# A decoder trunk with forgetting attention: norms of four token tiles at once, operand preparation in another place, masks first in their banks

## The chip, the cores and the metric

The kernel runs on one core of one Trainium2 chip. The metric is the device time of one execution in microseconds (us); smaller is better. All inputs are fp32, and the arithmetic keeps close to fp32: a dense product is emulated by three matmuls in a faster float form.

## The reference

```python
for l in range(DEPTH):                      # 2 layers, x is 512 tokens x 1024
    x = x + 0.5 * swiglu(rms_norm(x, ffn1_norm[l]), ffn1_w_in[l], ffn1_w_out[l])
    h = rms_norm(x, mix_norm[l]) @ w_mix_in[l]
    (c_x, c_b, c_c, h_q, h_f, h_i, h_g, f_q, f_k, f_v, f_f) = jnp.split(h, split_at, axis=-1)
    y = jnp.concatenate([
        short_conv_mixer(c_x, c_b, c_c, conv_w[l]),
        hgrn2_mixer(h_q, h_f, h_i, h_g, lower_bounds[l], hgrn_out_gain[l]),
        fox_mixer(f_q, f_k, f_v, f_f, fox_f_bias[l], fox_q_gain[l], fox_k_gain[l]),
    ], axis=-1)
    x = x + y @ w_mix_out[l]
    x = x + 0.5 * swiglu(rms_norm(x, ffn2_norm[l]), ffn2_w_in[l], ffn2_w_out[l])
...
# fox_mixer: 8 heads of 64, blocks of 128 queries
qh = rms_norm(heads(q), q_gain) * (HEAD_DIM ** -0.5)
kh = rms_norm(heads(k), k_gain)
cum = jnp.cumsum(jax.nn.log_sigmoid(f_logit + f_bias), axis=1)
s = einsum('bhqd,bhkd->bhqk', qb, kh) + (cb[..., :, None] - cum[..., None, :])
s = jnp.where(qpos[:, None] >= kpos[None, :], s, MASK_VALUE)
o = einsum('bhqk,bhkd->bhqd', jax.nn.softmax(s, axis=-1), vh)
```

The change touches `fox_mixer` alone: the norms of its queries and keys, the making of a head's operands, and the place of the causal mask within the scores.

## The kernel before

Each layer runs `ffn`, `mix`, `ffn`. A dense product splits both sides into a high and a low part (on the weights' side ACT casts the high part at L435, DVE takes the remainder at L438; buffers `st` for the weights as they come, two of them, and `hl` for the parts, three), and `mm3` issues three matmuls: high by high (L451), high by low (L457), low by high (L458). ACT is ScalarE, DVE VectorE, PE TensorE, POOL GpSimd, SP the engine whose queue issues most transfers.

`mix` has two stages that matter here.

In the first one two generators of `hgrn` (one for each pair of heads) run in turn with dense steps of `fox_qkv`; the table `HGRN_BESIDE` says how many dense steps stand between two steps of `hgrn`. `hgrn` computes its scores in three groups of levels: 64 small matmuls in `score` (L1494) write two banks tagged `sc`, DVE's `place` copies them under a mask into the matrix `A` (L1514), and before these copies it makes the operands of the next group (L1463, L1464, L1471). `fox_qkv` projects the queries and keys of four heads for one half `hf` of the heads, then of the other half, each into four banks (one for each tile of 128 tokens), copies a bank to `qk` (L1661) and queues one call of `norm(qk, i)` for each token tile in `later`. `beside` pops one such call after each dense step. `norm` takes the sum of squares of 8 vectors of 64 in each token row (Square on ACT at L1644, reduction on DVE at L1645), the inverse root by Ln and Exp on ACT and a correcting step (`rsqrt`, L597, L600, L601; with two scalings, L1646 and L1652), all on 128x8 elements, and scales the tile (L1655).

In the second stage `fox_attend` walks through 16 steps (h, p): head h, first (p = 0) or second (p = 1) half of the query blocks. A step does, before the change, in this order:

- `turn(h, p)`: transposes the weights of the step (3 blocks for p = 0, 7 for p = 1; L1772) into `pt` banks; ACT casts them to PH (L1777), DVE takes the remainder PL (L1778);
- `scores` of the step two ahead: for each query block a matmul of QA with KA and one of QB with KB into a bank `sc` (in these two matmuls lie the parts of the split and the two rows for the decay), and the causal mask, a bf16 matmul of an identity with `maskb`, added to the same bank (all L1735); then the maximum (L1749), Exp (L341), reciprocal (L1751) and the scaling of the weights (on ACT L1755 for p = 1, on DVE L1757 for p = 0);
- `values` of the step before: PH and PL against V into the one bank `po` (L1790); for p = 1 also the sum into `fo` (L1803, L1804), and for an odd head the parts `fyh` on ACT (L1807) and `fyl` on DVE (L1808), operands of the output projection;
- for p = 0, `prep` of head h + 2 (`fox_prep`): a two-row transfer (L1693), a POOL memset (L1694), four transposes of `qk` into a `pt` bank (L1697), the high part `hi` on ACT (L1700), the low part `lo` on DVE (L1701), and six transfers on SP that put their 64-row halves together to QA, KA, QB, KB (L1708).

Heads alternate between two sets of these operands: `S`, `q` for odd ones, `A`, `kb` for even ones. Between the steps run dense ones (the V and conv projections and most of the output projection), as many as the table `BESIDE` says. There are two banks `pt`, two `sc`, one `po`.

On PE `self.follow("p")` fixes the order of the matmuls of these steps as the program writes them. On the other engines the instructions stand in the order that a scheduler gives them, with what the program writes first ahead where both can go. Each engine then works its queue off in order.

## Time and profile before

| | |
|---|---|
| three runs | 1764.95, 1764.04, 1764.25 us; median 1764.25 |
| the profiled execution's own time | 1765.45 us |
| its span in the profile | 1763.3 us |
| granted TensorE clock | 1.00 of full speed |
| first stage of `mix`, layer 0 / layer 1 | about 384 to 446 / 1250 to 1318 us |
| second stage (`fox_attend`) | about 446 to 558 / 1318 to 1430 us |
| PE busy in these four stretches | 61.77 of 62, 110.86 of 112, 67.77 of 68, 111.55 of 112 us |

In the rows below a line such as L1735 is a line of the kernel before; buffer numbers are left out of names. "sc<-q,q" means that the instruction reads two buffers q and writes the bank sc. "PEld" is PE's loading of weights, which overlaps the matmuls. PE's matmuls are pipelined: a row's duration is longer than the distance to the next start, and that distance is what the matmul costs. A bracket behind a row is the idle time ahead of it and what ended it.

### The profile page before, as it was taken

The numbers are of one execution on the slowest core, as the hardware profiler recorded it, in microseconds if no ns is written. First come the engines' busy times: TensorE is split into PE (matmuls) and PEld (weight loads), VectorE is DVE, ScalarE is ACT, GpSimd is POOL, SyncE is SP. The second block draws the span as 40 slices with busy tenths as digits, with TensorE's granted clock in tenths as the row PEclk, the third lists the DMA queues.
The fourth block names the chain that finished last, engine by engine and source line by source line (L and its number), as shares of the span: only waits on it lengthen the run. The fifth ranks groups of instructions, "written<-read, shape, count | busy, mean of one in ns | idle before, by whom it ended". The sixth has DMA issues, their size and how long they took to land.

```text
span 1763.3 us, 33430 instructions
## 1 busy us (share of the span) xinstructions
PE 1753.8 (99%) x13613; PEld 1643.2 (93%) x13613; DVE 1416.0 (80%) x1956; ACT 1015.8 (58%) x1433; POOL 177.0 (10%) x174
## 2 busy tenths in 40 slices
PE   9999999999999999999999999999999999999999
PEld 7999999888888899999989999998888889999998
DVE  7988788679777898888679787876888779888783
ACT  5465555466666565555446656555657655655652
POOL 0011120100000111112001111201000001120200
PEclk9999999999999999999999999999999999999999
DMA  7768784243543776869267787923435438687762
GB/s 202 188 140 199 180 177 111 73 124 82 132 118 99 216 163 161 202 169 178 81 183 170 178 182 176 192 79 79 120 93 134 123 103 220 156 176 195 162 138 96
DMA packets 257465, 262.34 MB, mean 149 GB/s; under 512 B 25832, under 2 KB 236528, under 8 KB 257312
## 3 DMA queue, kind: packets, MB, share of 16 engines
q1 hardware_dynamic: 201456, 192.02, 36.4%
q0 software_dynamic: 55840, 68.19, 24.0%
q8 instruction: 107, 1.75, 0.4%
q14 instruction: 46, 0.38, 0.1%
q10 hardware_dynamic: 16, 0.00, 0.0%
HBM read 226.15 MB, written 2.17 MB: 129 GB/s over the span
## 4 chain that ended last, share of the span: by engine, by line
PE 90%; DVE 6%; ACT 2%; issue 1%; DMA 1%; SPq 0%; ACTq 0%; DVEq 0%
PE mm L451 12%; PE mm L458 12%; PE mm L457 12%; PE sc L458 6%; PE sc L451 6%; PE sc L457 6%; PE pt L457 6%; PE pt L451 6%; PE pt L458 6%; PE po L451 3%; PE po L458 3%; PE po L457 3%; DVE hl L438 1%; PE sc L1735 1%; PE po L1790 1%; PE pt L1772 1%
## 5 line engine op out<-in xcount | busy, mean ns | idle before, releaser
L916 DVE TENSOR_TENSOR hl<-w,hl 128x1024 fp32r<-128x1024 f32 x279 | 341.0, 1223 | 91.0 <-ACT hl L914 89.5
L914 ACT CAST hl<-w 128x1024 fp32r<-128x1024 f32 x279 | 292.6, 1049 | 198.3 <-PE mm L458 56.0
L438 DVE TENSOR_TENSOR hl<-st,hl 128x1024 fp32r<-128x1024 f32 (+3 forms) x152 | 160.4, 1056 | 103.0 <-ACT hl L435 101.4
L435 ACT CAST hl<-st 128x1024 fp32r<-128x1024 f32 (+3 forms) x151 | 137.4, 910 | 160.9 <-PE po L458 61.7
L451 PE MATMUL mm<-xc,hl 128*128 128x256 f32 x698 | 191.6, 275 | 0.6 <-ACT u L1034 0.6
L458 PE MATMUL mm<-xc,hl 128*128 128x256 f32 x696 | 191.6, 275 | 0.0
L457 PE MATMUL mm<-xc,hl 128*128 128x256 f32 x696 | 191.5, 275 | 0.0
L451 PE MATMUL pt<-xc,hl 128*128 128x256 f32 x546 | 149.7, 275 | 0.0
L457 PE MATMUL pt<-xc,hl 128*128 128x256 f32 x544 | 149.7, 275 | 0.0
L458 PE MATMUL pt<-xc,hl 128*128 128x256 f32 x544 | 149.6, 275 | 0.0
L451 PEld LDWEIGHTS mm<-xc,hl 128*128 128x128 f32 x698 | 133.9, 192 | 0.9 <-ACT u L1034 0.8
L458 PEld LDWEIGHTS mm<-xc,hl 128*128 128x128 f32 x696 | 133.6, 192 | 0.4 <-DVE hl L916 0.4
L457 PEld LDWEIGHTS mm<-xc,hl 128*128 128x128 f32 x696 | 133.6, 192 | 0.0
L458 PE MATMUL sc<-xc,hl 128*128 128x256 f32 x464 | 127.8, 275 | 0.1
L451 PE MATMUL sc<-xc,hl 128*128 128x256 f32 (+1 forms) x466 | 127.8, 275 | 0.0
L457 PE MATMUL sc<-xc,hl 128*128 128x256 f32 x464 | 127.7, 275 | 0.0
L451 PE MATMUL mm<-x,hl 128*128 128x512 f32 x272 | 105.9, 390 | 0.0
L451 PEld LDWEIGHTS pt<-xc,hl 128*128 128x128 f32 x546 | 104.7, 192 | 0.0
L457 PEld LDWEIGHTS pt<-xc,hl 128*128 128x128 f32 x544 | 104.4, 192 | 0.0
L458 PEld LDWEIGHTS pt<-xc,hl 128*128 128x128 f32 x544 | 104.4, 192 | 0.0
L457 PE MATMUL mm<-x,hl 128*128 128x512 f32 x272 | 103.1, 379 | 0.0
L458 PE MATMUL mm<-x,hl 128*128 128x512 f32 x272 | 103.1, 379 | 0.0
(520 smaller groups left out, 5595.9 us busy)
## 6 DMA issues: line engine op xcount, KB each, us to landing
w<-in_ffn_w_in_dram SPq DMA_DIRECT2D x124, 512.0 KB, 6.0
w<-in_ffn_w_out_dram POOLq DMA_DIRECT2D x50, 512.0 KB, 9.6
w<-in_ffn_w_out_dram SPq DMA_DIRECT2D x49, 512.0 KB, 4.5
st<-in_ffn_w_out_dram SPq DMA_DIRECT2D x39, 512.0 KB, 3.8
st<-in_w_mix_in_dram SPq DMA_DIRECT2D x72, 256.0 KB, 3.0
st<-in_ffn_w_in_dram SPq DMA_DIRECT2D x70, 256.0 KB, 3.5
w<-in_ffn_w_in_dram POOLq DMA_DIRECT2D x29, 512.0 KB, 10.1
w<-S POOLq DMA_DIRECT2D x29, 512.0 KB, 5.1
```

Of the source, the lines that this page charges most:

```text
L435: a = nc.scalar.copy(hi, src[:, c : c + w])
L438: b = nc.vector.tensor_sub(lo, src[:, c : c + w], hi)
L451: i = nc.tensor.matmul(acc[:, c], ah, bh[:, c.start // 2 : c.stop // 2, :], start=first and c.start == 0, stop=False, skip_group_check=True,)
L457: nc.tensor.matmul(acc, ah, bl, start=False, stop=False, skip_group_check=True)
L458: i = nc.tensor.matmul(acc, al, bh, start=False, stop=last, skip_group_check=True)
L914: A(nc.scalar.copy(hi, src))
L916: return lambda: V(nc.vector.tensor_sub(lo, src, hi))
L1735: mm = lambda *a, **k: E(nc.tensor.matmul(*a, skip_group_check=True, **k))
L1772: E(nc.tensor.transpose(tb[:, k * P : (k + 1) * P], to[u][:, j * P : (j + 1) * P], self.ident))
L1790: E(nc.tensor.matmul(self.ob[:, o], half[2][:, j, h].rearrange("p a d -> p (a d)"), part[:, at[0] : at[-1] + 1, :].rearrange("p b t -> p ( ...
```

## The change

There are three edits. `norm(qk, i)` becomes `norms(qk)`: four calls that take the squares and sums of one token tile each, the last of them with the small steps for all four tiles on 128x32 elements, and two calls that scale two tiles each; all six are queued at once when `qk` is filled. In `fox_attend` a head's `prep` stands right behind `turn`, before `scores` and `values`. In `scores` the mask matmuls come first and open the bank, for p = 1 both of them ahead of the other four.

```diff
--- before.py
+++ after.py
@@ -1635,24 +1635,35 @@
                     later.pop(0)()
                 yield
 
-        def norm(qk, i):
-
-            x = qk[:, i].rearrange("p h w d -> p (h w) d")
-            sq = hp.tile([P, 8, HD], F32, tag="fs", name=self.n("fs"))
-            s8 = lambda tag: mp.tile([P, 8], F32, tag=tag, name=self.n(tag), bufs=2)
-            m, r, t = s8("fm"), s8("fr"), s8("ft")
-            nc.scalar.activation(sq, x, AF.Square)
-            nc.vector.reduce_sum(m, sq, axis=AX.X)
-            nc.vector.tensor_scalar(
-                m, m, scalar1=self.inv2[:, i : i + 1], scalar2=None, op0=ALU.mult
-            )
-            self.act(r, m, AF.Ln, bias=self.epsc)
-            self.act(r, r, AF.Exp, scale=-0.5)
-            self.rsqrt(r, m, r, t)
-            nc.vector.tensor_scalar(
-                r, r, scalar1=self.invc[:, i : i + 1], scalar2=None, op0=ALU.mult
-            )
-            nc.vector.tensor_mul(x, x, r.unsqueeze(2).to_broadcast([P, 8, HD]))
+        def norms(qk):
+
+            small = lambda tag: mp.tile([P, 4, 8], F32, tag=tag, name=self.n(tag), bufs=2)
+            m, r, t = small("fm"), small("fr"), small("ft")
+            wide = lambda a: a.unsqueeze(2).to_broadcast([P, 4, 8])
+
+            def squares(i):
+                x = qk[:, i].rearrange("p h w d -> p (h w) d")
+                sq = hp.tile([P, 8, HD], F32, tag="fs", name=self.n("fs"))
+                nc.scalar.activation(sq, x, AF.Square)
+                nc.vector.reduce_sum(m[:, i], sq, axis=AX.X)
+
+            def finish():
+                nc.vector.tensor_mul(m, m, wide(self.inv2))
+                self.act(r, m, AF.Ln, bias=self.epsc)
+                self.act(r, r, AF.Exp, scale=-0.5)
+                self.rsqrt(r, m, r, t)
+                nc.vector.tensor_mul(r, r, wide(self.invc))
+
+            def scale(i):
+                x = qk[:, i].rearrange("p h w d -> p (h w) d")
+                nc.vector.tensor_mul(x, x, r[:, i].unsqueeze(2).to_broadcast([P, 8, HD]))
+
+            later.append(lambda: squares(0))
+            later.append(lambda: squares(1))
+            later.append(lambda: squares(2))
+            later.append(lambda: (squares(3), finish()))
+            later.append(lambda: (scale(0), scale(1)))
+            later.append(lambda: (scale(2), scale(3)))
 
         for hf in range(2):
             qk = mp.tile([P, 4, 4, 2, HD], F32, tag="qk", name=self.n("qk"), bufs=2)
@@ -1662,7 +1673,7 @@
                     qk[:, i].rearrange("p h w d -> p w h d"),
                     bank.rearrange("p (h d w) -> p w h d", w=2, h=4),
                 )
-                later.append(lambda qk=qk, i=i: norm(qk, i))
+            norms(qk)
             half.append(qk)
         V = mp.tile([P, 4, NH, 2, HD], F32R, tag="V", name=self.n("V"))
         half.append(V)
@@ -1729,20 +1740,19 @@
                 at = [b[:, :P], b[:, P : 3 * P]]
             else:
                 at = [self.bank("sc")[:, : 3 * P], self.bank("sc")]
+            mm = lambda *a, **k: E(nc.tensor.matmul(*a, skip_group_check=True, **k))
+            if p == 0:
+                masked = [b.rearrange("p (b t) -> p b t", t=P)[:, ::2, :]]
+            else:
+                masked = [at[u][:, (2 + u) * P : (3 + u) * P] for u in range(2)]
+            for m in masked:
+                mask = self.maskb.unsqueeze(1).to_broadcast([P, 2, P]) if p == 0 else self.maskb
+                mm(m, self.identb, mask, start=True, stop=False)
             for u in range(2):
                 i = 2 * p + u
                 c, n = slice(i * P, (i + 1) * P), (i + 1) * P
-                mm = lambda *a, **k: E(nc.tensor.matmul(*a, skip_group_check=True, **k))
-                mm(at[u], QA[:, c], KA[:, :n], start=p == 1 or u == 0, stop=False)
-                mm(at[u], QB[:, c], KB[:, :n], start=False, stop=False)
-                if p == 1:
-                    mm(at[u][:, c], self.identb, self.maskb, start=False, stop=True)
-                elif u == 1:
-
-                    mm(
-                        b.rearrange("p (b t) -> p b t", t=P)[:, ::2, :], self.identb,
-                        self.maskb.unsqueeze(1).to_broadcast([P, 2, P]), start=False, stop=True,
-                    )
+                mm(at[u], QA[:, c], KA[:, :n], start=False, stop=False)
+                mm(at[u], QB[:, c], KB[:, :n], start=False, stop=True)
             to = [pb[:, :P], pb[:, P:]] if p == 0 else [pb[:, : 3 * P], pb[:, 3 * P :]]
             for u in range(2):
                 o = slice(u, u + 1)
@@ -1817,12 +1827,12 @@
         yield
         for k, (h, p) in enumerate(steps):
             turn(h, p)
+            if p == 0 and h + 2 < NH:
+                prep(h + 2)
             if k + 2 < len(steps):
                 scores(*steps[k + 2])
             if k:
                 values(*steps[k - 1])
-            if p == 0 and h + 2 < NH:
-                prep(h + 2)
             yield
         values(*steps[-1])
 
```

The number of instructions on PE stays the same, on SP and POOL too; per layer DVE has 34 fewer rows and ACT 18 fewer. In the three places below the rows have the line, the operation, and out<-in with shapes; behind L1635 the lines of the changed kernel are up to 11 higher (L1735 has become L1743, L1697 L1708, L1700 L1711, L1772 L1782, L1777 L1787, L1755 L1765, L1790 L1800, L1803 L1813, L1807 L1817, L1655 L1659 and L1652 L1655).

First place: PE in `fox_attend`, the step (0, 1) with the scores of (1, 1). `pt` holds the turned weights, `sc` are the two banks of scores, S and q the operands of head 1. Before:

```order
L1772 MATMUL pt_5389<-ident,P_5288 128x128 x3
L1735 MATMUL sc_5398<-S_655_5216,S_654_5215 128x384
L1735 MATMUL sc_5398<-q_657_5218,q_656_5217 128x384
L1735 LDWEIGHTS identb
L1735 MATMUL sc_5398<-maskb,identb 128x128
L1735 MATMUL sc_5399<-S_655_5216,S_654_5215 128x512
L1735 MATMUL sc_5399<-q_657_5218,q_656_5217 128x512
L1735 LDWEIGHTS identb
L1735 MATMUL sc_5399<-maskb,identb 128x128
L1790 MATMUL po_5413<-PH_5324,V_4848 128x256
```

And of the change:

```order
L1782 MATMUL pt_5323<-ident,P_5222 128x128 x3
L1743 LDWEIGHTS identb
L1743 MATMUL sc_5332<-maskb,identb 128x128
L1743 LDWEIGHTS identb
L1743 MATMUL sc_5333<-maskb,identb 128x128
L1743 MATMUL sc_5332<-S_637_5150,S_636_5149 128x384
L1743 MATMUL sc_5332<-q_639_5152,q_638_5151 128x384
L1743 MATMUL sc_5333<-S_637_5150,S_636_5149 128x512
L1743 MATMUL sc_5333<-q_639_5152,q_638_5151 128x512
L1800 MATMUL po_5347<-PH_5258,V_4818 128x256
```

Both masks now stand between the transposes and the first score matmul. In a step with p = 0 the four transposes of the new head's `prep` stand between the transposes of `turn` and the mask, where before they closed the step.

Second place: DVE in the first stage of layer 0, at the third group of the first pair's scores. `fr` and `ft` hold the factors of the norms, `t` the operands of `hgrn`, `hl` the parts of a dense step's weights. Before:

```order
L597 SCALAR_TENSOR_TENSOR ft_4635<-fm_4633,ft_4635 128x8
L1463 TENSOR_TENSOR t_4689<-kb_3705,b_3703 128x16x16
L600 TENSOR_SCALAR ft_4635<-ft_4635 128x8
L1464 TENSOR_TENSOR t_4689<-b_3703 128x16x16
L601 TENSOR_TENSOR fr_4634<-fr_4634,ft_4635 128x8
L438 TENSOR_TENSOR hl_4855<-st_4853,hl_4855 128x1024
L1652 TENSOR_SCALAR fr_4634<-fr_4634,invc_3901 128x8
L1514 COPY_PREDICATED A_4325<-lmask,sc_4647 128x64x2
L1655 TENSOR_TENSOR qk_4158<-qk_4158,fr_4634 128x512
L1514 COPY_PREDICATED A_4325<-lmask,sc_4648 128x64x2
L1471 TENSOR_TENSOR t_4685<-t_4689,q_3707 128x256
```

And of the change:

```order
L601 TENSOR_TENSOR fr_4474<-fr_4474,ft_4475 128x32
L1464 TENSOR_TENSOR t_4652<-b_3703 128x16x16
L1655 TENSOR_TENSOR fr_4474<-fr_4474,invc_3901 128x32
L1463 TENSOR_TENSOR t_4727<-kb_3704,b_3702 128x8x32
L1659 TENSOR_TENSOR qk_4158<-qk_4158,fr_4474 128x512
L1471 TENSOR_TENSOR t_4648<-t_4652,q_3707 128x256
L1659 TENSOR_TENSOR qk_4158<-qk_4158,fr_4474 128x512 x3
L438 TENSOR_TENSOR hl_4825<-st_4823,hl_4825 128x1024
L1514 COPY_PREDICATED A_4325<-lmask,sc_4610 128x64x2
L1514 COPY_PREDICATED A_4325<-lmask,sc_4611 128x64x2
```

The scalings of the four token tiles now stand together, ahead of the copies to `A` with an operand (L1471) among them, and an operand of the next group (L1463) stands ahead of them too; before, one scaling stood between two copies. The dense remainder (L438) keeps its place just ahead of the copies.

Third place: ACT in `fox_attend` of layer 0, where `fo` of heads 2 and 3 is completed. `P` are the weights of the softmax, `b_800` and `b_777` the high part that `prep` makes. Before:

```order
L1777 CAST PH_5865<-pt_5867 128x384
L1755 ACTIVATE P_5818<-P_5818,rs_5820 128x384
L1755 ACTIVATE P_5818<-P_5818,rs_5820 128x512
L341 ACTIVATE P_5873,rs_5875<-sc_5876,nm_5874 128x128
L1803 COPY t_5897<-po_5836 64x512
L341 ACTIVATE P_5873,rs_5875<-sc_5876,nm_5874 128x256
L1700 ACTIVATE b_800_5902<-pt_5909,qkg_3687 128x512
L1807 CAST fyh_636_5142<-fo_5749 128x512
```

And of the change:

```order
L1787 CAST PH_5799<-pt_5801 128x384
L1765 ACTIVATE P_5752<-P_5752,rs_5754 128x384
L1765 ACTIVATE P_5752<-P_5752,rs_5754 128x512
L1711 ACTIVATE b_777_5807<-pt_5814,qkg_3687 128x512
L341 ACTIVATE P_5827,rs_5829<-sc_5830,nm_5828 128x128
L1813 COPY t_5851<-po_5770 64x512
L341 ACTIVATE P_5827,rs_5829<-sc_5830,nm_5828 128x256
L1817 CAST fyh_618_5072<-fo_5704 128x512
```

The high part of the next operands (L1700, now L1711) stands ahead of the two exponentials and of the copy out of `po` (L1803, now L1813); before, it stood behind them. On DVE the low part (L1701, now L1712) moves, in most steps, ahead of the reductions of the same scores in the same way.

## The prediction

> **What bounds the kernel now.** I read the page first, then the list of what TensorE (PE) waited for, then the two stages that the change touches.
>
> ```profile
> PE 1753.8 (99%) x13613; PEld 1643.2 (93%) x13613; DVE 1416.0 (80%) x1956; ACT 1015.8 (58%) x1433; POOL 177.0 (10%) x174
> PE 90%; DVE 6%; ACT 2%; issue 1%; DMA 1%; SPq 0%; ACTq 0%; DVEq 0%
> ```
>
> The first row is busy time, the second the chain that ended last. PE sets the end: work taken off VectorE (DVE) or ScalarE (ACT) is worth only what PE stops waiting for. From PE's list of waits these rows matter (us in total, times, longest):
>
> ```profile
> PE mm L457 <- DVE fyl L1808: 0.9, 2, 0.4
> PE sc L1494 <- DVE A L1514: 0.4, 2, 0.2
> ```
>
> Each occurs twice, once per layer. A matmul's shown duration overlaps the next one's, so these sums understate the loss; below I count from start to start. The span of 1763.3 us in the table above, plus about 2 us around it, is the profiled execution of 1765.45 us, 1.2 us over the median of the runs, 1764.25. The sum is a difference, so I take it off either.
>
> **Norms at once.** PE's timeline of layer 0 (start, us, what), then two rows of the chain:
>
> ```profile
> 421.82 0.38 PE L451 MATMUL po<-hl,x 128*128 128x512 f32 x1
> 422.04 0.38 PE L457 MATMUL po<-hl,x 128*128 128x512 f32 x1
> 422.25 0.38 PE L458 MATMUL po<-hl,x 128*128 128x512 f32 x1
> 422.82 1.33 PE L1494 MATMUL sc<-t,t 64*64 64x32 f32 x64 [0.19 <-DVE A L1514]
> 424.08 0.48 PE L451 MATMUL mm<-hl,x 128*128 128x512 f32 x1
> ...
> 429.53 1.06 PE sc L1494 x64
> ```
>
> A dense 512-column matmul takes 0.22 us from start to start. The last one before the HGRN scores took 0.57, so PE lost 0.35 us; the 64 score matmuls then took 1.26, the next 64 only 1.06, as the second score bank was still being placed by DVE. Together 0.55; I call it 0.5 us per layer. Everywhere else in this stage PE runs at its pace, so 0.5 is all that lighter norms can bring.
>
> Do they bring it? Per half, five kinds of small DVE steps run once on 32 columns and not four times on 8: fifteen instructions go, and eight wide ones (four sums of squares, four scalings) stay. The timeline of DVE:
>
> ```profile
> 412.54 0.16 DVE L601 TENSOR_TENSOR fr<-fr,ft 128x8 f32<-128x8 f32 x1
> 412.62 0.23 DVE L1646 TENSOR_SCALAR fm<-fm,inv 128x8 f32<-128x8 f32 x1
> 412.75 1.22 DVE L438 TENSOR_TENSOR hl<-st,hl 128x1024 fp32r<-128x1024 f32 x1
> ```
>
> A small step holds DVE for 0.08 to 0.13 us, so fifteen free 1.2 to 2.0 us ahead of the four L1514 that PE waits for. Against that the new order puts two HGRN operands (L1463 and L1471) ahead of them, some 0.6 us by the dense neighbours of 0.3. The copies come 0.6 to 1.4 us earlier, and 0.5 is enough: minus 0.5 per layer, **minus 1.0 in all**, cover for it being DVE time that was saved in the same queue. If the four scalings, now bunched right ahead of the copies, find their factors late (they wait for ACT's Ln, Exp and Square), up to 1 us per layer would be lost. So this term lies between minus 1.0 and plus 2.0; the new order has four copies and an operand split between the first small step and the next, so I stay at minus 1.0. In the second half nothing covers the step from the first factor to ACT and back, yet PE showed no wait there. The 18 ACT instructions that go per layer free nothing that PE waits for.
>
> **A head's operands earlier.** In layer 0 one set of scores waited for its operand transfers:
>
> ```profile
> 476.92 0.59 PE sc L1735 x5
> 477.51 0.89 PE po L1790 x8
> 478.40 0.46 PE pt L1697 x4
> ```
> ```profile
> 486.20 0.49 PE L1772 MATMUL pt<-ident,P 128*128 128x128 f32 x3
> 487.03 0.30 PE L1735 MATMUL sc<-S,S 128*128 128x128 f32 x1 [0.34 <-DMA S<-b]
> 487.68 0.30 PE L1735 MATMUL sc<-q,q 66*128 66x128 f32 x1 [0.35 <-DMA q<-b]
> 487.81 0.34 PE L1735 MATMUL sc<-S,S 128*128 128x256 f32 x1
> ```
>
> Three transposes at 0.11 us would have let the scores start at 486.53; they started at 487.03, and their first matmul took 0.65 where the next took 0.13. That is 1.0 us lost, in layer 0 alone. The four transposes of this head (L1697) stood behind the scores (0.59) and values (0.89). They now stand ahead, so the cast L1700, the remainder L1701 and the seven transfers on the SP queue start up to 1.48 us sooner. That exceeds 1.0: **minus 1.0**, with zero as the other end, if ACT holds the cast back. What is late next is L1701 itself and the softmax of the next scores, which now stands behind L1700 on ACT and L1701 on DVE. PE needs those weights only two steps later. The SP queue gets one weight load and one two-row transfer in another place; the load goes behind the seven transfers of head 5. Two staging buffers and three split buffers stand between it and PE, so I cost it at nothing; without that cover it would cost the 0.6 us a transfer takes to issue times seven, 4 us, per layer. On PE the four transposes cost 0.46 us where they are and four times 0.11 behind others of their kind, plus a switch saved or added: plus or minus 0.3 over twelve places, taken as zero.
>
> The second wait of the list stands in the way of that ACT and DVE pair:
>
> ```profile
> 514.33 0.68 DVE L1349 TENSOR_TENSOR cu<-mm,inv 128x512 f32<-128x512 f32 x1
> ...
> 515.15 0.59 ACT b L1700
> 515.92 0.56 DVE b L1701
> 516.49 0.54 DVE P L1757 x2
> 517.03 0.61 DVE fyl L1808
> ```
> ```profile
> 516.86 0.38 PE L451 MATMUL mm<-fyh,hl 128*128 128x512 f32 x1
> 517.68 0.48 PE L457 MATMUL mm<-fyl,hl 128*128 128x512 f32 x1 [0.45 <-DVE fyl L1808]
> ```
>
> PE lost 0.82 less 0.22, 0.6 us, waiting for fyl. The rows before it are ACT without a gap, so moving L1700 forward in that row does not shorten the row. The last exponential now ends 0.59 later, and behind it come the reciprocal, L1349 (it stood before), both L1757 and fyl: from about 515.8, 0.1 + 0.65 + 0.54 gives fyl a start of 517.1 to 517.3, not 517.03. I take 0.2 us more per layer: **plus 0.4**, between minus 1.2 (the wait goes) and plus 1.2 (the whole 0.59).
>
> **Masks first.** The steps of a second half of queries, then of a first half:
>
> ```profile
> 481.98 0.42 PE L1735 MATMUL sc<-A 128*128 128x384 f32 x1
> 482.24 0.34 PE L1735 MATMUL sc<-kb,kb 66*128 66x384 f32 x1
> 482.42 0.23 PE L1735 MATMUL sc<-maskb,identb 128*128 128x128 bf16 x1
> 482.46 0.48 PE L1735 MATMUL sc<-A 128*128 128x512 f32 x1
> 482.78 0.40 PE L1735 MATMUL sc<-kb,kb 66*128 66x512 f32 x1
> 483.02 0.10 PEld L1735 LDWEIGHTS <-identb 128*128 128x128 bf16 x1 [0.28 <-issue]
> 483.02 0.23 PE L1735 MATMUL sc<-maskb,identb 128*128 128x128 bf16 x1
> 483.06 0.37 PE L1790 MATMUL po<-PH,V 128*128 128x256 f32 x1
> ...
> 500.47 0.28 PE L1735 MATMUL sc<-maskb,identb 128*128 128x256 bf16 x1
> 500.51 0.37 PE L1790 MATMUL po<-PH,V 128*128 128x256 f32 x1
> 500.71 0.28 PE L1790 MATMUL po<-PL,V 128*128 128x256 f32 x1
> 500.83 0.28 PE L1790 MATMUL po<-PH,V 128*128 128x256 f32 x1
> ```
>
> A mask takes 0.04 us, but the matmul behind it pays: 512 columns in 0.32 and not 0.22, 256 in 0.20 and not 0.12; and the one ahead pays 0.02. Two masks between float matmuls cost 0.16 + 0.14 = 0.30 us. The first float matmul behind the transposes pays the same 0.10 today (0.26 for 384 columns, against 0.16). With the masks between, that payment stays, and added are the last transpose's rest (0.03 to 0.08 of its 0.11 spacing), 0.02, and two masks of 0.04 to 0.10: 0.13 to 0.24. A second half saves 0.06 to 0.17, I take 0.12. A first half has one mask, costing 0.13 today, and its first matmul of 128 columns pays behind the mask too: from 0.05 saved to 0.06 lost, I take 0.03 lost. Sixteen of each: **minus 1.4**, between minus 3.5 and zero.
>
> The Trainium skill, "TensorE: Matmul & The Clock Gate", section "Step-by-step: what each phase is for", says that the reorder window pulls weight loads ahead of running matmuls, so that a load hides wherever it stands. By it this term would be zero. The row of 483.02 disagrees, since the identity's load began only with its mask after 0.28 us of idle; no run yet shows a mask behind transposes.
>
> **The sum**: -1.0 - 1.0 + 0.4 - 1.4 = -3.0 us. The profiled execution would go from 1765.45 to 1762.5, the median from 1764.25 to **1761.3**.
>
> **Rivals.** First: the masks' place is indifferent, the 0.30 being only moved to the transposes. For it: a switch to float is paid once anyway, and nothing shows transposes ahead of a mask. Against: two masks then share one switch. Sum -1.6, 1762.7. The skill's rule above gives the same.
>
> Second, slower: the cast that moved forward holds up the softmax. In each of the twelve moved places L1700 (0.59) now stands ahead of the exponentials on ACT. Where ACT has no gap, fo, fyh, fyl and the next weights' split come 0.59 later, and so does PE: 12 x 0.59 = 7.1, less the 3.0, gives 1768.4. It decides from the point where half the places expose it. For it: the gapless ACT row before 517.03. Against: only one of the six places per layer shows PE waiting today, and
>
> ```profile
> 446.00:558.00 112.00, 110.86 (x635) 96.00 (x636) 84.51 (x159) 75.62 (x159) 3.10 (x6) 1.00 0.47 123
> ```
>
> ACT is busy 75.62 of this stage's 112 us (fourth figure after the stretch).
>
> Third, faster: masks at their best end (-3.5) and the fyl waits gone (-1.2), with both -1.0 terms: -6.7, 1757.6. The two small gains would have to hold and the ACT row to shorten, which nothing shows.
>
> Fourth, the norms do not do what they should: the bunched scalings keep the 0.5 us waits. Then -2.0, 1762.3.
>
> **How the numbers follow.** Forecast 0.45, masks indifferent 0.17, softmax held up 0.15, faster 0.15, norms idle 0.08. A difference under 0.2%, 3.5 us, is about what a measurement of this kernel can tell from no change, so the line for faster is 1760.7 and for slower 1767.8. The forecast stands 0.6 us from that line: of its 0.45 I give 0.20 to faster. With the third rival and a little of the others faster is 0.37; slower is 0.14, the second rival where it decides; same is 0.49. The forecast's own range is 1758.8 to 1763.5; to leave out no more than two in ten the range goes from 1757.3 to 1767.6, about the third rival's time and most of the way to the second.
>
> **What would show it.** Right: no wait of L1494 for L1514 at the third group of scores; no wait of scores for transfers in layer 0; a 512-column score matmul at 0.22 and the first value matmul at 0.12; a fyl wait of 0.6 to 0.9 in both layers. Wrong: any new PE wait on PH, PL or hl between the first and last scores; a transpose ahead of a mask that takes more than 0.15 us; DVE idle in front of the scalings. Outside the two stages nothing should move.

## The result, and the profile after

The changed kernel takes 1761.89 us (median of 22 runs, 1760.50 to 1763.09), the kernel before 1764.17 us (22 runs): 2.28 us less, a ratio of 0.9986 with a 95% interval from 0.9980 to 0.9992. 1761.3 was forecast. The difference is 0.13%, under the 0.2% that was called no change, and its interval excludes 1.

The profiled execution of the changed kernel has a span of 1760.2 us, 3.1 less than before. To see where they lie I take three marks in each layer from PE's timeline: the first matmul of the HGRN states (L1424), the matmul of the HGRN output's mean of squares (L1582), and the first matmul of the next norm (L535). Before, then after, for layer 0 (start, us, what):

```profile
388.53 0.69 PE L1424 MATMUL pt<-v,t 64*64 64x64 f32 x32
...
444.85 0.70 PE L1582 MATMUL sc<-t,ones_blk 128*128 128x512 f32 x1
...
560.98 0.70 PE L535 MATMUL sc<-fyh,hl 128*128 128x512 f32 x2 [0.24 <-ACT fyh L1807]
```
```profile
387.58 0.69 PE L1424 MATMUL pt<-v,t 64*64 64x64 f32 x32
...
443.24 0.70 PE L1582 MATMUL sc<-t,ones_blk 128*128 128x512 f32 x1
...
558.12 0.48 PE L535 MATMUL sc<-fyh,hl 128*128 128x512 f32 x1 [0.24 <-ACT fyh L1817]
```

Between the marks lie the first stage (56.32 us before, 55.66 after) and the second (116.12 and 114.88 here; differences of the unrounded starts can be 0.01 off). Layer 1, read in the same way, gives 56.21 and 55.73, then 115.01 and 114.89. So the two stages give -0.66, -1.24, -0.48 and -0.12, together -2.50 us. The other -0.6 us lies in the untouched parts. These add up to anything from 1418.2 to 1421.3 us in the executions of this document, so a stage tells more than a span here.

PE's list of waits (us in total, times, longest) says what the numbers are made of:

```profile
PE mm L457 <- DVE fyl L1818: 1.4, 2, 0.7
PE sc L535 <- ACT fyh L1817: 0.5, 2, 0.2
```

The wait of the HGRN scores for A and both waits for transfers are gone. The wait for fyl has grown from 0.9 to 1.4. The list also has a new wait of 1.2 us for L438, at 9.4 us in the start-up. It costs nothing: with the moved prep alone (below) PE starts that matmul at 9.39 too, without a wait.

**Norms.** The place where PE had waited for A, in the changed kernel, PE and then DVE:

```profile
421.14 0.38 PE L458 MATMUL po<-hl,x 128*128 128x512 f32 x1
421.45 1.13 PE L1494 MATMUL sc<-t,t 64*64 64x32 f32 x64
422.52 0.48 PE L451 MATMUL mm<-hl,x 128*128 128x512 f32 x1
```
```profile
416.94 1.89 DVE L1659 TENSOR_TENSOR qk<-qk,fr 128x512 f32<-128x512 f32 x3
418.75 1.22 DVE L438 TENSOR_TENSOR hl<-st,hl 128x1024 fp32r<-128x1024 f32 x1
419.88 1.06 DVE L1514 COPY_PREDICATED A<-lmask,sc 128x128 f32<-128x128 uint8 x4
```

The 64 score matmuls take 1.07 us from start to start, as the undisturbed ones did. They start 0.31 us after the last dense matmul, without a bracket; before it was 0.57 us. (So the pace there is 0.31, not the 0.22 that the prediction took, and 0.26 us was lost there, not 0.35.) All four copies end at 420.94, half a microsecond before PE wants the bank. One sign that the prediction called wrong did show, DVE idle in front of the scalings. It stands in the second half's norms, where the small steps wait for ACT:

```profile
434.25 0.19 DVE L597 SCALAR_TENSOR_TENSOR ft<-fm,ft 128x32 f32<-128x32 f32 x1 [0.91 <-ACT ft L341]
```

PE does not wait for A there either, so this idle time cost nothing.

**Masks.** A step of a second half of queries:

```profile
480.10 0.60 PE L1782 MATMUL pt<-ident,P 128*128 128x128 f32 x4
480.53 0.28 PE L1743 MATMUL sc<-maskb,identb 128*128 128x128 bf16 x2
480.62 0.42 PE L1743 MATMUL sc<-A 128*128 128x384 f32 x1
480.88 0.34 PE L1743 MATMUL sc<-kb,kb 66*128 66x384 f32 x1
481.05 0.40 PE L1743 MATMUL sc<-A 128*128 128x512 f32 x1
481.29 0.40 PE L1743 MATMUL sc<-kb,kb 66*128 66x512 f32 x1
481.52 0.28 PE L1800 MATMUL po<-PH,V 128*128 128x256 f32 x1
481.64 0.28 PE L1800 MATMUL po<-PL,V 128*128 128x256 f32 x1
```

A 512-column score matmul costs 0.24 us where it cost 0.32, the first value matmul 0.12 where it cost 0.20. The two masks take 0.09 us together, and four transposes ahead of them take 0.43, so that the last one keeps its 0.11, where it had taken 0.03 before.

**A new loss.** PE at the scores of head 2, the first operands made in the moved place, and of head 3; then what the list for L1743 says of PE's weight-load queue between 474 and 478 us (x4 instructions, shortest/median/longest ns, first and last start):

```profile
475.01 0.60 PE L1708 MATMUL pt<-ident,qk 128*128 128x128 f32 x4
475.44 0.27 PE L1743 MATMUL sc<-maskb,identb 128*128 128x256 bf16 x1
475.59 0.30 PE L1743 MATMUL sc<-A 128*128 128x128 f32 x1
475.82 0.30 PE L1743 MATMUL sc<-kb,kb 66*128 66x128 f32 x1
475.96 0.33 PE L1743 MATMUL sc<-A 128*128 128x256 f32 x1
...
485.33 0.27 PE L1743 MATMUL sc<-maskb,identb 128*128 128x256 bf16 x1
485.36 0.31 PE L1743 MATMUL sc<-S,S 128*128 128x128 f32 x1
485.50 0.28 PE L1743 MATMUL sc<-q,q 66*128 66x128 f32 x1
```
```profile
L1743 PEldq EVENT_SEMAPHORE  x4: 51/51/51, 475.4 to 475.7; - x4
```

The mask takes 0.15 us to the next start and the first matmul with A 0.23; at head 3 they take 0.03 and 0.14. About 0.2 us is lost, in both layers at the same head, and no bracket names a wait. The time is spent around four semaphore instructions (instructions that only wait for a semaphore): two run between the mask and the first matmul with A, two more between that one and the matmul with kb. In layer 0 the transfers that they wait for had all landed by 473.63, by the trace's landing events, so no transfer was late. The semaphore instructions stand there because of what waits for what. PE's instructions at this place with the semaphores that each waits for, before and after (DMAHW: transfers, Activation: ACT, Pool: POOL):

```
before
L1735 MATMUL sc_5457<-A_5350 128x128 [waits DMAHW6_49,DMAHW2_49,DMAHW7_49,DMAHW0_49,Activation_49]
L1735 MATMUL sc_5457<-kb_682_5352,kb_681_5351 128x128 [waits DMAHW3_49,DMAHW4_49,DMAHW1_49,Pool_49]
after
L1743 LDWEIGHTS identb
L1743 MATMUL sc_5412<-maskb,identb 128x2x128 [waits Activation_49]
L1743 MATMUL sc_5412<-A_5268 128x128 [waits DMAHW6_49,DMAHW7_49,DMAHW2_49,DMAHW0_49]
L1743 MATMUL sc_5412<-kb_660_5270,kb_659_5269 128x128 [waits DMAHW3_49,DMAHW4_49,DMAHW1_49,Pool_49]
```

The Activation wait is for the Exp that last read this bank. Before, the first matmul with A carried it itself, behind the semaphore instructions of its transfers. Now the mask carries it, and all four stand behind the mask. Here the Exp is late:

```profile
475.13 0.19 ACT L341 ACTIVATION_READ_ACCUMULATOR P<-sc,nm 128x1 f32 x1
475.25 0.69 ACT L341 ACTIVATE P<-sc,nm 128x512 f32<-128x512 f32 x1
```

Its sum has been read at 475.32, and the semaphore instructions begin right behind that, at 475.37. Before, it was read 0.06 us ahead of the step's first transpose; now it is 0.64 us behind it.

**The fyl wait.** ACT, DVE and PE at the end of fo of heads 2 and 3:

```profile
513.23 0.62 ACT L1817 CAST fyh<-fo 128x512 fp32r<-128x512 f32 x1
```
```profile
513.31 0.67 DVE L1349 TENSOR_TENSOR cu<-mm,inv 128x512 f32<-128x512 f32 x1
513.89 0.54 DVE L1767 TENSOR_SCALAR P<-P,rs 128x128 f32<-128x128 f32 x2
514.35 0.68 DVE L1818 TENSOR_TENSOR fyl<-fo,fyh 128x512 fp32r<-128x512 f32 x1
```
```profile
514.01 0.38 PE L451 MATMUL mm<-fyh,hl 128*128 128x512 f32 x1
515.09 0.48 PE L457 MATMUL mm<-fyl,hl 128*128 128x512 f32 x1 [0.69 <-DVE fyl L1818]
```

PE loses 1.08 less 0.22, 0.86 us, in either layer, where it lost 0.61. L1349 and the two scalings stand between fo and fyl as they did; all begin later, since the cast of prep(6) is now ahead of the exponentials.

### The profile page after: what moved, and what is told of

Read it like the earlier page. It is cut to its first block, busy times and chain, and to the rows that moved or that the text cites. A ratio compares the mean times of both kernels' runs of the same rounds, so it can differ in the third digit from the quotient of the medians.

```text
span 1760.2 us, 33346 instructions
## 1 busy us (share of the span) xinstructions
PE 1750.0 (99%) x13613; PEld 1644.6 (93%) x13613; DVE 1409.1 (80%) x1896; ACT 1009.9 (57%) x1397; POOL 177.3 (10%) x174
## 4 chain that ended last, share of the span: by engine, by line
PE 85%; DVE 7%; DMA 3%; issue 2%; ACT 2%; SPq 0%; POOL 0%; ACTq 0%; DVEq 0%; POOLq 0%
PE mm L451 12%; PE mm L457 12%; PE mm L458 12%; PE pt L457 6%; PE pt L451 6%; PE pt L458 6%; PE sc L458 6%; PE sc L451 6%; PE sc L457 5%; PE po L451 3%; PE po L457 3%; PE po L458 3%; DVE hl L438 2%; PE sc L1743 1%; PE pt L1782 1%
## 5 line engine op out<-in xcount | busy, mean ns | idle before, releaser
L438 DVE TENSOR_TENSOR hl<-st,hl 128x1024 fp32r<-128x1024 f32 (+3 forms) x152 | 160.0, 1053 | 102.0 <-ACT hl L435 100.6
```

What stands on the lines that cost most here:

```text
L438: b = nc.vector.tensor_sub(lo, src[:, c : c + w], hi)
```

## The experiments

For each kernel the table has the two stages of both layers between the marks above (us, one profiled execution each) and the median of its runs with that of the kernel before from the same job.

| kernel | first stage, layer 0 / 1 | second stage, layer 0 / 1 | median | before |
|---|---|---|---|---|
| before | 56.32 / 56.21 | 116.12 / 115.01 | 1764.17 | |
| changed | 55.66 / 55.73 | 114.88 / 114.89 | 1761.89 | 1764.17 |
| norms only | 55.74 / 55.72 | 116.44 / 114.88 | 1762.54 | 1764.43 |
| small steps by tile | 56.78 / 56.77 | 114.88 / 114.91 | 1764.81 | 1764.43 |
| masks only | 56.15 / 56.38 | 114.96 / 114.44 | 1762.24 | 1764.43 |
| prep only | 56.25 / 56.27 | 115.30 / 115.30 | 1763.60 | 1764.43 |
| prep, odd heads | 55.72 / 55.64 | 114.38 / 114.38 | 1761.08 | 1764.63 |
| the same again | 55.68 / 55.69 | 114.89 / 114.40 | 1761.17 | 1764.66 |
| mask half | 55.75 / 55.68 | 114.77 / 114.76 | 1761.84 | 1764.63 |
| values first | 55.69 / 55.66 | 116.59 / 116.65 | 1765.18 | 1764.63 |
| values first, odd prep | 55.66 / 55.79 | 115.96 / 116.00 | 1763.97 | 1764.63 |
| changed, again | 55.71 / 55.66 | 114.92 / 114.93 | 1762.24 | 1764.66 |
| values first, head 4, odd prep | 55.74 / 55.66 | 114.34 / 113.81 | 1759.47 | 1764.66 |
| values first, head 4 | 55.66 / 55.66 | 114.05 / 114.05 | 1760.10 | 1764.55 |

A stage that a kernel doesn't touch repeats within about 0.2 us, apart from the second stage of layer 0 wherever the operands come late. Medians of one kernel differ by up to 0.5 us between jobs. The stages are what the verdicts rest on.

**Norms only.** The kernel before with `norms` (as in the change) in place of `norm`:

```diff
-                later.append(lambda qk=qk, i=i: norm(qk, i))
+            norms(qk)
```

> The kernel before with the first edit alone (norms of four token tiles at once). My theory, DVE is late with the copies to A and the edit makes it early: the wait of the HGRN scores for A goes in both layers, the first stage (from the first U matmul to the mean-of-squares matmul) gets 0.5 to 0.65 us shorter in each, the second stage does not move, total -1.1 us against before. Rival, the bunched scalings keep the copies late and the gain came from elsewhere in the full change: the 0.35 us wait stays and the total is within 0.3 us of before.

The first stages are 0.58 and 0.49 us shorter, and the wait for A is in neither layer. The second stage of layer 1 moved by -0.13, that of layer 0 by +0.32, which the wait for transfers more than covers: head 3's step took 3.83 us in this execution, 3.39 before and 2.27 without a wait. My theory holds; -1.89 us by the median is more than these stages show.

**Small steps by tile.** The changed kernel, with the four tiles' small steps one after the other:

```diff
             def finish():
-                nc.vector.tensor_mul(m, m, wide(self.inv2))
-                self.act(r, m, AF.Ln, bias=self.epsc)
-                self.act(r, r, AF.Exp, scale=-0.5)
-                self.rsqrt(r, m, r, t)
-                nc.vector.tensor_mul(r, r, wide(self.invc))
+                for i in range(4):
+                    a, b, c = m[:, i], r[:, i], t[:, i]
+                    nc.vector.tensor_scalar(
+                        a, a, scalar1=self.inv2[:, i : i + 1], scalar2=None, op0=ALU.mult
+                    )
+                    self.act(b, a, AF.Ln, bias=self.epsc)
...
```

> The full change, but the small steps of the norms run once for each token tile on 128x8 again (30 small DVE steps and 18 small ACT instructions more per layer); the six calls and their places stay. If the number of small steps made DVE late: 1.2 to 2.0 us more DVE time in the stretch that had about 0.6 us to spare, so the wait of the scores for A comes back with 0.5 to 1.0 us per layer, total +1 to +2 us against the full change. If it was the order (scalings ahead of the copies and not between them): no wait, total within 0.3 us of the full change.

Each first stage is 1.1 us longer than in the changed kernel, so the small steps cost at least what the first theory said (2.2 us in all by the stages, where 1 to 2 was expected). The place is another than the one I had in mind. The third group of scores, where PE had waited before the change, shows no wait. It stands one group later, at the copies behind the second half's norms, here PE and then DVE:

```profile
437.46 0.38 PE L458 MATMUL po<-hl,x 128*128 128x512 f32 x1
438.65 0.57 PE L1494 MATMUL sc<-t,t 64*64 64x32 f32 x13 [0.81 <-DVE A L1514]
```
```profile
434.50 0.24 DVE L597 SCALAR_TENSOR_TENSOR ft<-fm,ft 128x8 f32<-128x8 f32 x2
434.65 0.23 DVE L1653 TENSOR_SCALAR fm<-fm,inv 128x8 f32<-128x8 f32 x1
434.79 0.24 DVE L600 TENSOR_SCALAR ft<-ft 128x8 f32<-128x8 f32 x2
...
437.43 0.23 DVE L1659 TENSOR_SCALAR fr<-fr,invc 128x8 f32<-128x8 f32 x1
437.69 0.69 DVE L1665 TENSOR_TENSOR qk<-qk,fr 128x512 f32<-128x512 f32 x1
438.30 0.49 DVE L1514 COPY_PREDICATED A<-lmask,sc 128x128 f32<-128x128 uint8 x2
```

DVE is busy from 434.5 to these copies with small steps between the scalings, and PE loses 1.19 less 0.22, 0.97 us. So two things are shown. The new order is enough for the third group: there three scalings stand ahead of the copies and one behind, none between, though the copies end only 0.13 us before PE starts (421.22 and 421.35; with the joined steps 0.5). And the joined steps are what keeps the last group free once the calls are bunched.

**Masks only.** The kernel before with the masks first, as in the change:

```diff
+            for m in masked:
+                mask = self.maskb.unsqueeze(1).to_broadcast([P, 2, P]) if p == 0 else self.maskb
+                mm(m, self.identb, mask, start=True, stop=False)
...
-                if p == 1:
-                    mm(at[u][:, c], self.identb, self.maskb, start=False, stop=True)
```

> The kernel before with the third edit alone (masks open the banks). My theory, two masks share one switch: a step of a second half takes 0.08 us less on PE (8 per layer), a step of a first half 0.03 less, so -0.8 to -0.9 us per layer, -1.7 us in all; the layer 0 wait of 1.0 us for the operands of head 5 stays, and so does the fyl wait of 0.6 us in both layers. Rival, the masks' place is indifferent and the switch is only moved: 0 us, 512-column score matmuls faster but the transposes slower by the same.

The second stage of layer 1 is 0.57 us shorter. Taking a step from its first transpose to the second dense matmul behind it, less one spacing of 0.22, second halves go from 2.31 to 2.22 us on average (seven in the layer with values), and an undisturbed first half from 2.27 to 2.245. So the place is not indifferent. The scores of head 2 lose 0.18 us in this layer and none in layer 0. Here the mask and the Exp are on time; the fourth semaphore instruction comes 0.17 us later than in layer 0, though its transfers had landed, and why stays open. At the scores of head 5, where the Exp is read 0.17 us behind the first transpose, some 0.07 us is lost in both layers, so a loss of this kind needs no moved prep. The head whose operands come late in layer 0 is head 3, not 5 as the expectations say; its wait was 0.6 us here, against 1.1 before and 1.55 with norms only.

**Prep only.** The kernel before with `prep` behind `turn`:

```diff
             turn(h, p)
+            if p == 0 and h + 2 < NH:
+                prep(h + 2)
...
-            if p == 0 and h + 2 < NH:
-                prep(h + 2)
```

> The kernel before with the second edit alone (prep behind turn). My theory: the layer 0 wait for operands goes (-1.0 us), the fyl wait grows from 0.6 to 0.85 us in both layers (+0.5), the four transposes cost 0 to 0.04 us more in each of twelve steps (+0 to +0.5), and the scores of head 2, which in the full change started 0.2 us late in both layers, do so here too (+0.4): total -0.5 to +0.4 us. Rival, that late start comes from the mask ahead of the scores and not from the moved prep: no such loss here, total -0.5 to 0. Rival, the wait for operands was one slow transfer and comes and goes by itself: then it stands here too or at another head, total +0.5 to +1.4.

There is no wait for transfers in layer 0 (-0.82 us in its second stage), and the scores of head 2 lose nothing, so the first rival holds for that loss: the moved prep alone doesn't make it, though the Exp is late here too (read 0.50 us behind the first transpose). The fyl wait is 0.80 us and not 0.61. The second stage of layer 1, where no operand was late before, is 0.29 us longer: 0.19 for fyl, 0.1 for the six moved sets of transposes. The median alone could not tell this kernel from the one before (ratio 0.9994, 0.9986 to 1.0003).

**Prep, odd heads.** The changed kernel with early `prep` only for odd h:

```diff
             turn(h, p)
-            if p == 0 and h + 2 < NH:
+            if p == 0 and h % 2 and h + 2 < NH:
                 prep(h + 2)
             if k + 2 < len(steps):
                 scores(*steps[k + 2])
             if k:
                 values(*steps[k - 1])
+            if p == 0 and h % 2 == 0 and h + 2 < NH:
+                prep(h + 2)
```

> The full change, but prep stands behind turn only in steps of odd heads, and at the end of the step, as before the change, in steps of even heads. My theory of the new 0.2 us loss at the scores of head 2: PE's weight-load queue stands at the mask until the Exp two steps back has read the bank, and four semaphore instructions for the operands' transfers (0.11 us each) stand behind the mask; moved prep makes that Exp late. Here prep(2) does not delay it, so the loss goes (-0.2 us per layer), and the cast of prep(6) is no longer ahead of the exponentials at the fyl wait, which goes from 0.86 back to 0.6 us (-0.25 per layer); the operands of head 5 are still early, no wait in layer 0. Total -0.9 to -1.1 us against the full change. Rival, the loss at head 2 is a transfer that lands late: prep(2) later makes it 0.5 us or more, and the total is 0 to +0.5.

Both second stages are 0.5 us shorter than in the changed kernel: head 2 loses nothing, and the fyl wait is 0.59 and 0.62. The rival falls. A loss of 0.1 us at the scores of head 5 has come instead, with the Exp 0.18 us behind the first transpose. In the second execution,

> The kernel with prep behind turn in steps of odd heads only, a second time: 0.9 to 1.1 us under the changed kernel of this batch if the gain seen in its profile (0.5 us in each second stage) is one of the time too; a difference under 0.5 us would say that the median cannot show it.

the median is 1.07 us under the changed kernel's of that job, but the scores of head 3 lost 0.45 us in layer 0. Prep(2), late again, also makes prep(3) late: its cast starts 2.67 us behind the step's first transpose, against 1.61 in the changed kernel, though its place in the program is the same.

**Mask half.** The changed kernel with the mask last again in first halves only:

```diff
-            for m in masked:
...
+            if p:
+                for u in range(2):
+                    m = at[u][:, (2 + u) * P : (3 + u) * P]
+                    mm(m, self.identb, self.maskb, start=True, stop=False)
...
+            if p == 0:
+                mm(
+                    b.rearrange("p (b t) -> p b t", t=P)[:, ::2, :], self.identb,
+                    self.maskb.unsqueeze(1).to_broadcast([P, 2, P]), start=False, stop=True,
+                )
```

> The full change, but steps of a first half have their one mask last again; second halves have the masks first. By my theory of the semaphore instructions behind the mask, the 0.2 us loss at the scores of head 2 goes in both layers (-0.4 us), and the other seven first-half steps of a layer give back 0.03 us each (+0.4): total within 0.2 us of the full change. Rival, Exp or a transfer is late for the bank whatever opens it: the loss stays and the total is +0.4 us.

The total is as expected, the size at head 2 is not: its step takes 2.41 us, against 2.50 in the changed kernel and 2.28 without the loss. Two of the semaphore instructions now run ahead of A, but the Exp is as late as it was. So the order accounts for somewhat under half of the loss here. With the masks first and the Exp early (masks only) it was 0.18 us in one layer, at another place in the step, and none in the other; with the old order and the Exp 0.50 us late (prep only) none; the full 0.2 us in both layers came only with both.

**Values first.** The changed kernel with `values` ahead of `scores` in first halves:

```diff
+            if k and p == 0:
+                values(*steps[k - 1])
             if k + 2 < len(steps):
                 scores(*steps[k + 2])
-            if k:
+            if k and p == 1:
                 values(*steps[k - 1])
```

> The full change, with values ahead of scores in the steps of first halves (turn, prep, values, scores). If the fyl wait (0.86 us in each layer) is made by what stands ahead of fo, fyh and fyl on ACT and DVE, the copies of the values now come ahead of the two exponentials and of both scalings: the wait goes in both layers, -1.7 us, and the loss at head 2 goes with it (the scores start 0.9 us later in the step), -0.4: total -1.8 to -2.2 us against the full change. Rival, scores that come 0.9 us later make the weights late two steps on: new waits of PE for PH or of the turn for P, total 0 to +2.

The rival holds, with another wait than it named: each second stage is 1.7 us longer. The values went ahead, but the wait for fyl is still 0.7, since the cast of prep(6) stands ahead of the copy out of `po`. The later exponentials hold the bank:

```profile
489.71 0.22 PE L1743 MATMUL sc<-maskb,identb 128*128 128x128 bf16 x1
491.68 0.22 PE L1743 MATMUL sc<-maskb,identb 128*128 128x128 bf16 x1 [1.75 <-ACT P L341]
```

PE's second mask waits for the Exp of the step before to leave one of the two banks `sc`, 1.9 us at this step in both layers.

**Values first, odd prep.** Both of these edits.

> Both of these together: values ahead of scores in first halves, prep behind turn only in steps of odd heads. Fyl wait and the loss at head 2 go as in the kernel with values first; prep at the end of a step costs 0.03 us less on PE in three steps of a layer: total -1.9 to -2.3 us against the full change. If late weights or late operands come of it (prep of an even head now starts 0.9 us later than before the change), a wait of scores for transfers shows, +0.5 to +1.5 against the kernel with values first.

The fyl wait shrinks to about 0.1 us, the step with the wait for the bank loses 1.4 us (1.1 between its two masks), and a wait of 0.66 us for xT (L1285) comes behind: second stages 1.1 us longer than in the changed kernel. The steps around heads 2 and 3 do the harm, far from where the fyl wait is.

**Changed, again; values first at head 4.** The first is the changed kernel beside the others, the second has values ahead of scores in one step only (k = 8), with prep in odd heads.

> The changed kernel itself, on the same chip as the two below, to have their differences from it directly: 2.3 us under before, head 2 loses 0.2 us and the fyl wait is 0.85 us in both layers.

> The same with values ahead of scores in one step alone, that of head 4's first half, behind which PE waits for fyl. If the losses of the kernel with values first everywhere came from the other steps, the fyl wait goes (0.6 to 0.1 us) and nothing takes its place: -1.0 us against prep in odd heads. If DVE is full there and the wait only moves: a wait of PE for xT (L1285) of 0.6 to 0.7 us behind it in both layers, as values first with odd prep showed, total within 0.3 us of prep in odd heads.

The changed kernel repeats (-2.42 us). With values first at one step the fyl wait is gone in both layers and no wait for xT comes. The second stage of layer 1 is 1.08 us shorter than in the changed kernel; in layer 0 head 3 lost 0.5 us to late transfers. Its median, 1759.47, is the lowest here, from 6 runs: ratio to before 0.9968 (0.9956 to 0.9980).

**Values first at head 4 alone.** With what the runs had shown, every other `prep` went back behind `turn`:

```diff
             turn(h, p)
-            if p == 0 and h + 2 < NH:
+            if p == 0 and h != 4 and h + 2 < NH:
                 prep(h + 2)
+            if k == 8:
+                values(*steps[k - 1])
             if k + 2 < len(steps):
                 scores(*steps[k + 2])
-            if k:
+            if k and k != 8:
                 values(*steps[k - 1])
+            if p == 0 and h == 4:
+                prep(h + 2)
```

> The full change with one step alone altered, the first half of head 4: values ahead of scores there, and prep(6) at its end; all other preps stay behind turn. By the prices so far: the fyl wait goes in both layers (-0.86 us each), the 0.2 us loss at the scores of head 2 stays, and since prep(2) is early the scores of head 3 do not wait for transfers in layer 0 (the three kernels with prep(2) late lost 0, 0.45 and 0.5 us there): each second stage 0.8 to 0.95 us shorter than with the full change, total -1.6 to -1.9 us against it, so 1760.2 to 1760.7. If the wait for the transfers of head 3 is chance and has nothing to do with how early prep stands: 0.4 us or more lost there in layer 0.

Each second stage is 0.83 us shorter than in the changed kernel, the median 1760.10 us: ratio to before 0.9976 (0.9966 to 0.9985). Head 3 does not wait, and this is fyl's place:

```profile
513.20 0.68 DVE L1818 TENSOR_TENSOR fyl<-fo,fyh 128x512 fp32r<-128x512 f32 x1
```
```profile
514.10 0.38 PE L451 MATMUL mm<-fyh,hl 128*128 128x512 f32 x1
514.32 0.38 PE L457 MATMUL mm<-fyl,hl 128*128 128x512 f32 x1
514.53 0.38 PE L458 MATMUL mm<-fyh,hl 128*128 128x512 f32 x1
```

fyl is done at 513.88, 0.44 us ahead of the matmul that needs it. This kernel and the one with odd prep beat both the kernel before and the changed one. For this one the second half rests on the stages and on runs of different jobs: its slowest run took 1760.73 us, and only one of the changed kernel's 33 was as fast. Which of the two is better their runs don't settle.

## Why the prediction was right, step by step

The time came out 0.6 us over the forecast, inside its own range (1758.8 to 1763.5). By terms, from the stages of the changed kernel and the single edits:

| term | forecast | measured |
|---|---|---|
| norms at once | -1.0 | -1.14 (alone -1.07) |
| operands of head 3 in time | -1.0 | -1.1 |
| fyl later | +0.4 | +0.5 |
| masks | -1.4 | -1.5 |
| moved transposes | 0, up to 0.3 either way | +0.2 |
| head 2's scores behind the mask | none | +0.45 |
| sum | -3.0 | -2.6 (the four stages: -2.50) |

*Norms.* The size held. The reason given, "DVE time that was saved in the same queue", was half of it: bunching alone freed the third group, by 0.13 us, and without the joined steps the bunched order would have lost 1 us per layer at the last group, a place the prediction passed over with "yet PE showed no wait there".

*Operands.* Right: in every kernel with prep(2) and prep(3) behind turn no score waited for transfers, in the three with both late the wait was 0.6, 1.1 and 1.55 us, and in the three with prep(2) alone late (values first everywhere left out) 0, 0.45 and 0.5. The trace's landing events show why it was layer 0 alone, and that the size was that of one execution. A transfer lands in sixteen parts. In layer 1 all parts of head 3's transfers land together (within 0.1 us, before and after). In layer 0 the sixteenth part of some comes 1 to 2 us behind the others, in thirteen of the fourteen executions, the changed kernel's too, and where prep(3) is late one issue on SP can be slow besides. Counted in us from the first transpose of the step ahead, that of head 2's scores:

| kernel, layer | first issue | slowest issue takes | last part has landed | head 3's step begins | lost |
|---|---|---|---|---|---|
| before, 1 | 4.40 | 0.60 | 9.83 | 9.77 | 0 |
| before, 0 | 4.41 | 1.85 | 11.11 | 9.77 | 1.1 |
| norms only, 0 | 4.39 | 1.84 | 11.55 | 9.76 | 1.55 |
| prep odd, again, 0 | 3.39 | 0.59 | 10.48 | 9.69 | 0.45 |
| changed, 0 | 2.34 | 0.60 | 9.65 | 9.89 | 0 |

So before the change there was no room for any delay. The moved prep issues 2.07 us sooner, more than the 1.48 of the prediction, and the late part lands 0.24 us before the step begins. That the delay cost just 1.0 us in the profiled execution was luck.

*fyl.* Right in place and sign; the cost was 0.25 and not 0.2 us per layer, and prep alone made 0.19 of it.

*Masks.* The sum was right through two errors that offset. A second half saves 0.08 to 0.09 us, not 0.12, and an undisturbed first half saves some 0.02 (masks only) where 0.03 lost was taken. The rule of the Trainium skill weighed there ("TensorE: Matmul & The Clock Gate", section "Step-by-step: what each phase is for") describes the weight load well: behind the transposes the two masks follow at 0.09 us together, and their loads begin at 480.43, while the transposes run, so they do hide. That section gives conditions for it; "wherever it stands" was the prediction's own. The gain shows in the float matmul behind each mask (0.24 for 0.32 us), which that rule doesn't speak of. Why that matmul is slow stays open: it may be the change of type, or its own weight load, shown with 0.19 us, that a mask of 0.04 us is too short to cover. No run here separates the two.

*What was missed*, the 0.45 us at head 2, is the step "what is late next". It looked for waits on PH, PL and hl two steps on, and there were none. It didn't ask which instruction now stands first at the bank, what that waits for, and what is queued behind it on PE.

*Rivals.* That the masks' place is indifferent falls with the masks alone. The softmax held up by the cast, at 0.59 us in every place, didn't come: only head 2 and fyl saw it. The third rival needed the fyl waits gone, and they grew; the fourth falls with the norms alone. Values first shows that the danger behind the second was real: scores 0.9 us later cost 1.9 us at one step, through the bank and not through the weights.

The medians show -2.28 us and the stages -2.50, which lies inside the interval of the medians (1.4 to 3.5 us less).

## What to carry to other kernels

When an instruction is made the first to touch a bank, it inherits the wait for the bank's last reader. Where that reader is late, the semaphore instructions queued behind are paid on the path; look at the wait lists, not only at the order. A cheap operation can cost at its neighbour, as the masks did here, so put several side by side. Move a producer only where its consumer was late: of the six places in a layer, one paid (head 3, in one layer), and two cost (heads 2 and 6).

## What was not expected of the hardware

Semaphore instructions on PE's weight-load queue are shown with 51 ns, and four of them took 0.3 us from the first start to the last (475.4 to 475.7) where no other work hid them. SP needs about 0.6 us to issue a 64-row transfer, but a few take two or three times as long, in every profile, at no fixed transfer; before the change and after it (ns, shortest/median/longest). The last two rows are the SP queue in the kernel before, at head 3's operands in layer 0: the slow issue, and one of the usual length behind it.

```profile
L1708 SPq DMA_DIRECT2D q<-b x16: 467/590/1846, 459.8 to 1400.9; - x16
```
```profile
L1719 SPq DMA_DIRECT2D q<-b x16: 534/587/1353, 458.2 to 1395.3; - x16
```
```profile
482.69 1.85 SPq L1708 DMA_DIRECT2D q<-b  x1
484.63 0.54 SPq L1708 DMA_DIRECT2D S<-b  x1
```

What makes such an issue slow, and one of a transfer's sixteen parts late, was not tried.
